# Second mixer of a two-layer trunk: heads in chunks of 128 tokens instead of 64

## The chip, the cores and the metric

The kernel runs on one core of one Trainium2 chip. The metric is the device time of one execution in microseconds (us); the kernel before took 1258.96 us, the median of three runs (1255.95 to 1259.48). The engines are named as in the profile: PE is TensorE (matrix products), PEld its loading of the stationary operand, DVE is VectorE, ACT is ScalarE, POOL is GpSimd, SP is the queue that issues the transfers.

## The reference, cut to what matters

The reference is a decoder trunk of two layers over 512 tokens and a width of 1024. The first layer has a mixer of its own and a SwiGLU part, the second the mixer below and a SwiGLU part. The second mixer has eight heads of width 128; for each head it computes a gated linear recurrence in chunks of 64 tokens:

```python
H_CHUNK = 64
def hgrn2_chunkwise(q, k, v, log_f):
    ...
    b = jnp.cumsum(log_f, axis=3)             # within the chunk
    b_last = b[:, :, :, -1:, :]
    q_inter = q * jnp.exp(b)
    k_state = k * jnp.exp(b_last - b)
    q_intra = q * jnp.exp(b - b_last)
    scores = jnp.where(causal, einsum(q_intra, k_state), 0.0)
    intra = einsum(scores, v)
    U = einsum(k_state, v)                    # what a chunk adds to the state
    decay = jnp.exp(b_last)
    def step(s, inp):
        u_c, d_c = inp
        return d_c[..., None] * s + u_c, s
    _, s_prev = lax.scan(step, zeros, (U, decay))
    inter = einsum(q_inter, s_prev)
    return intra + inter
```

The result does not depend on the chunk's length, except for rounding: a longer chunk computes more of the same sums as scores and fewer through the state.

## The kernel before, in words

All activations stand with the features on the 128 partitions and the 512 tokens along the free axis. A weight product (`prod`, `full`) splits both operands into a high and a low part of a reduced fp32 type and makes three products of 128x512 for each block of 128 features; in the profile these are the `bmm` rows with `wh`, `wl` (the parts of a weight) and `xh`, `xl` (the parts of the input), here called the wide products. The weights come by DMA into `wraw`, ACT copies the high part (`wh`), DVE (sometimes POOL) subtracts it for the low part (`wl`).

The order of the instructions on every engine is written by the planner `Sched`: tasks (generators) give a time or an event at which they may go on, and the planner picks the next one by its own table of costs. On PE it counts `p*n/2300` us for a product (`mm`; p is 4 for fp32, n the columns, at least 128 of them for fp32, and 16 for one that runs `beside` another) and 0.107 for a transpose (`tp`). The order is fixed when the program is built; on the chip an engine only waits for semaphores.

In the second mixer (`mixer1`) the wide products make `f`, `q`, `g` and `v` for the heads in the order `ORDER`. A task `gates` turns `f` and `q` of a head into `em` (named `f` in the profile: keys times a decay), `d` (named `q`: queries times a decay, for the scores), `b` (queries times a decay, for the state) and `dec` (eight decays, one for a chunk). A task `heads` then runs `head` for one head after the other, between the wide products. `head` before the change has eight chunks of 64 tokens, two in each block of 128:

- scores: 8 products of 64x64 (`bm<-q,f`), two side by side in the halves of the array, masked by DVE into `sc` (named `n`);
- transposes of the keys: 4 of 128x128 (`bs<-p,f`), copied by ACT into `kst` (also named `n`);
- state products: 7 with 64 rows (`bs<-v,n`), and with them the states `st`, one copied by ACT, six updated by DVE;
- outputs: 8 products of scores and values (`bm<-v,n`) and 7 of states and queries (`bm<-st,b`), with 64 columns of the array each;
- the norm of the outputs on ACT, DVE and POOL, and 4 transposes back (`bm<-p,n`).

A product in fp32 appears as two rows in the profile, so 8 score products are 16 rows, a transpose as one.

Of the kernel before, what the change touches and what calls it, by code (L numbers as in the profile page):

```python
# [14 lines left out]
ALU = mybir.AluOpType  # L15
# [249 lines left out]
class Kernel:  # L265
# [470 lines left out]
    def mixer1(self, nxt):  # L736
# [120 lines left out]

        def head(h, em, d, b, dec, t4, t6):

            yield t4  # L860
            ps, key = yield from self.alloc("m")
            half = [(slice(64 * u, 64 * u + 64), [slice(128 * i + 64 * u, 128 * i + 64 * u + 64) for i in range(4)])
                    for u in range(2)]
            for i in range(4):
                for u, (pp, cc) in enumerate(half):
                    t = S.mm(ps[pp, cc[i]], em[:, cc[i]], d[:, cc[i]], after=t4, beside=u > 0)
            pk, keyk = yield from self.alloc("s")
            for i in range(4):
                c = slice(128 * i, 128 * i + 128)
                tk = S.tp(pk[:, c], em[:, c], self.ident)  # L870
            sc = self.pt("n0")
            yield S.on("v", t)
            i3 = lambda z, u: z.rearrange("p (i t) -> p i t", t=128)[half[u][0], :, half[u][0]]
            for u in range(2):
                t = S.tt(i3(sc, u), i3(ps, u), self.tri[half[u][0], half[u][0]].unsqueeze(1).broadcast_to([64, 4, 64]),
                         ALU.mult, after=t)
            self.free(key)
            kst = self.pt("n5")
            tk = S.act(kst, pk, after=tk)
# [6 lines left out]
            tst = {0: 0.0}  # L886
            pu = yield from self.allocs("s", 2)
            tu = {}
            for c in (0, 1, 3, 5, 2, 4, 6):
                pp = slice(64 * (c % 2), 64 * (c % 2) + 64)  # L890
                kc = slice(128 * (c // 2), 128 * (c // 2) + 128)
                tu[c] = S.mm(pu[c % 2][0][:, kc], kst[pp, kc], v[c // 2][pp, hc])
                if c == 0:
                    tst[1] = S.act(st[:, 0], pu[0][0][:, 0:128], after=tu[0])
            yield S.on("v", max(tst[1], tu[6]))
            for c in range(1, 7):
                u = pu[c % 2][0][:, 128 * (c // 2):128 * (c // 2) + 128]
                tst[c + 1] = S.stt(st[:, c], st[:, c - 1], dec[:, c:c + 1], u, ALU.mult, ALU.add,
                                   after=max(tu[c], tst[c]))
            for g in range(2):  # L900
                self.free(pu[g][1])
# [1063 lines left out]
```

## Time and profile before

| what | value |
|---|---|
| median of three runs | 1258.96 us (1255.95 to 1259.48) |
| profiled execution, its own time | 1261.67 us |
| its span, first to last instruction | 1259.8 us |
| mean granted clock of TensorE | 0.991 of full speed |
| PE busy | 1224.8 us, 97% of the span |
| DVE busy | 720.8 us, 57% |
| ACT busy | 532.1 us, 42% |
| POOL busy | 101.6 us, 8% |
| DMA | 87 GB/s over the span |

The sums and the chain come from the profiled execution, so sums are made against its 1261.67 us. A matrix product's end is modelled in the trace, and products overlap: a duration of 0.39 us stands for a product that is followed by the next after 0.23. What a product costs is read from start to start.

### The profile page before, as it was taken

The numbers are of one execution on the slowest core, as the hardware profiler recorded it, in microseconds if no ns is written. First come the engines' busy times: TensorE is split into PE (matmuls) and PEld (weight loads), VectorE is DVE, ScalarE is ACT, GpSimd is POOL, SyncE is SP. The second block draws the span as 40 slices with busy tenths as digits, with TensorE's granted clock in tenths as the row PEclk, the third lists the DMA queues.
The fourth block names the chain that finished last, engine by engine and source line by source line (L and its number), as shares of the span: only waits on it lengthen the run. The fifth ranks groups of instructions, "written<-read, shape, count | busy, mean of one in ns | idle before, by whom it ended". The sixth has DMA issues, their size and how long they took to land.

```text
span 1259.8 us, 17687 instructions
## 1 busy us (share of the span) xinstructions
PE 1224.8 (97%) x7135; PEld 1028.4 (82%) x7135; DVE 720.8 (57%) x1225; ACT 532.1 (42%) x824; POOL 101.6 (8%) x104
## 2 busy tenths in 40 slices
PE   9988799999999999999999999999999999999996
PEld 8866689888888888889977787779988888888886
DVE  7999786863344434447766456655743444344445
ACT  5675575543322223324555455545533322223232
POOL 2200010100000000000112123310000000000002
PEclk9998999999999999999999999999999999999998
DMA  6301015142333333332132231222133333333321
GB/s 217 101 27 35 2 37 173 52 124 78 117 100 101 98 90 98 101 100 85 55 98 67 68 100 51 69 87 81 51 117 99 102 101 100 95 91 100 101 67 67
DMA packets 35072, 110.18 MB, mean 87 GB/s; under 512 B 3760, under 2 KB 6192, under 8 KB 34992
## 3 DMA queue, kind: packets, MB, share of 16 engines
q1 hardware_dynamic: 34992, 109.06, 28.4%
q8 instruction: 56, 0.92, 0.3%
q14 instruction: 24, 0.20, 0.0%
HBM read 106.95 MB, written 2.10 MB: 87 GB/s over the span
## 4 chain that ended last, share of the span: by engine, by line
PE 83%; DVE 11%; ACT 3%; issue 1%; POOL 1%; DMA 0%; SPq 0%; DVEq 0%; ACTq 0%
PE bmm L136 76%; PE bm L136 4%; PE bs L136 3%; DVE wl L156 1%; DVE n L156 1%; DVE t L156 1%; DVE xc L168 1%; POOL rcol L158 1%; DVE xl L156 1%; DVE Y L156 1%; DVE X L156 1%; DVE n L168 1%; ACT wh L150 0%; DMA wraw<-in_W_dram 0%; DVE t L172 0%
## 5 line engine op out<-in xcount | busy, mean ns | idle before, releaser
L150 ACT ACTIVATE wh<-wraw 128x1024 fp32r<-128x1024 f32 (+2 forms) x198 | 199.7, 1010 | 453.7 <-PE bmm L136 352.7
L136 PE MATMUL bmm<-xh,wh 128*128 128x512 f32 (+1 forms) x1008 | 384.4, 381 | 0.4 <-DVE Y L156 0.4
L136 PE MATMUL bmm<-xh,wl 128*128 128x512 f32 (+1 forms) x1008 | 378.5, 375 | 0.0
L136 PE MATMUL bmm<-xl,wh 128*128 128x512 f32 (+1 forms) x1008 | 378.4, 375 | 0.0
L156 DVE TENSOR_TENSOR wl<-wraw,wh 128x1024 fp32r<-128x1024 f32 (+2 forms) x196 | 228.4, 1167 | 99.7 <-ACT wh L150 99.5
L136 PEld LDWEIGHTS bmm<-xh,wh 128*128 128x128 f32 x1008 | 190.6, 189 | 37.5 <-issue 3.7
L136 PEld LDWEIGHTS bmm<-xh,wl 128*128 128x128 f32 x1008 | 190.6, 189 | 34.1
L136 PEld LDWEIGHTS bmm<-xl,wh 128*128 128x128 f32 x1008 | 190.8, 189 | 31.9
L156 DVE TENSOR_TENSOR a<-bmm,n 128x512 f32<-128x512 f32 x86 | 59.1, 691 | 219.4 <-PE bmm L136 216.2
L136 PE MATMUL bmm<-gh,wh 128*128 128x512 f32 (+1 forms) x368 | 135.0, 367 | 0.0
L136 PE MATMUL bmm<-gl,wh 128*128 128x512 f32 (+1 forms) x368 | 134.8, 366 | 0.0
L136 PE MATMUL bmm<-gh,wl 128*128 128x512 f32 (+1 forms) x368 | 134.7, 366 | 0.0
L158 POOL TENSOR_TENSOR rcol<-rstat,mhalf 128x2 f32<-128x2 f32 (+1 forms) x12 | 13.4, 1117 | 824.4 <-DVE rstat L164 824.4
L136 PEld LDWEIGHTS bmm<-gh,wh 128*128 128x128 f32 x368 | 69.4, 189 | 11.4
L136 PEld LDWEIGHTS bmm<-gl,wh 128*128 128x128 f32 x368 | 69.4, 189 | 11.3
L136 PEld LDWEIGHTS bmm<-gh,wl 128*128 128x128 f32 x368 | 69.4, 189 | 11.1
L156 DVE TENSOR_TENSOR Y<-bmm,Y 128x512 f32<-128x512 f32 (+1 forms) x40 | 23.3, 584 | 81.6 <-PE bmm L136 81.6
L150 ACT ACTIVATE xh<-X,p 128x256 fp32r<-128x256 f32 (+1 forms) x56 | 30.0, 538 | 29.7 <-DVE X L156 27.2
L150 ACT ACTIVATE n<-Y 128x256 f32<-128x256 f32 (+1 forms) x52 | 24.1, 464 | 43.5 <-DVE Y L156 42.4
L150 ACT ACTIVATE gh<-a 128x512 fp32r<-128x512 f32 x44 | 27.8, 632 | 25.9 <-DVE a L156 25.9
L148 ACT ACT_TABLE_LOAD x28 | 35.9, 1283 | 0.5
L156 DVE TENSOR_TENSOR n<-n,n 128x256 f32<-128x256 f32 (+1 forms) x44 | 23.5, 533 | 21.2 <-ACT n L150 20.9
(343 smaller groups left out, 1682.7 us busy)
## 6 DMA issues: line engine op xcount, KB each, us to landing
wraw<-in_W_dram SPq DMA_DIRECT2D x173, 512.0 KB, 3.6
wraw<-in_W_dram SPq DMA_DIRECT2D x16, 384.0 KB, 3.1
wraw<-in_W_dram SPq DMA_DIRECT2D x18, 256.0 KB, 3.0
X<-in_x_dram SPq DMA_DIRECT2D x16, 256.0 KB, 4.7
out_dram<-X SPq DMA_DIRECT2D x8, 256.0 KB, 2.2
setb<-in_s5bc_dram SPq DMA_DIRECT2D x1, 512.0 KB, 6.5
p<-in_p_dram SPq DMA_DIRECT2D x1, 226.5 KB, 6.4
n<-in_wif_dram SPq DMA_DIRECT2D x1, 192.0 KB, 4.3
```

What stands on the lines that cost most here:

```text
L136: self.nc.tensor.matmul(out, lhsT=lhsT, rhs=rhs, start=start, stop=stop, skip_group_check=True)
L148: self.nc.scalar.preload_act_table_set(t)
L150: self.nc.scalar.activation(out=out, in_=in_, func=func, scale=scale, bias=bias)
L156: self.nc.vector.tensor_tensor(out=out, in0=in0, in1=in1, op=op)
L158: self.nc.gpsimd.tensor_tensor(out=out, in0=in0, in1=in1, op=op)
L168: self.nc.vector.scalar_tensor_tensor(out=out, in0=in0, scalar=scalar, in1=in1, op0=op0, op1=op1)
```

## The change

Each head of the second mixer now works in four chunks of 128 tokens. The decays of a head are still computed by halves of 64. The scores within each half stay as they were; the cross scores of the second half against the first are four more products (`bm<-b,f`, 64x64), with the queries `b` that already hold the decay from the start of their half. The keys of the first half are scaled by the decay of the second half in place before they are transposed (three blocks, since the last chunk gives no state that is used), the queries of the second half by the decay of the first half, and the decay of a whole chunk (`whole`) is the product of two. Three states stand in place of seven. The state products and the outputs are full 128x128 products. The tile `sc` is made once for all heads; POOL fills the quarter of it that stays zero.

```diff
--- before.py
+++ after.py
@@ -855,61 +855,67 @@
                 yield from head(h, *hd.pop(h))
                 S.signal(("hd", h), 0.0)
 
+        sc = self.pt("n0")
+        S.zero(sc.rearrange("p (i t) -> p i t", t=128)[64:128, :, 0:64])
+
         def head(h, em, d, b, dec, t4, t6):
+
 
             yield t4
             ps, key = yield from self.alloc("m")
-            half = [(slice(64 * u, 64 * u + 64), [slice(128 * i + 64 * u, 128 * i + 64 * u + 64) for i in range(4)])
-                    for u in range(2)]
+            lo, hi = slice(0, 64), slice(64, 128)
+            cut = lambda i, w: slice(128 * i + w.start, 128 * i + w.stop)
             for i in range(4):
-                for u, (pp, cc) in enumerate(half):
-                    t = S.mm(ps[pp, cc[i]], em[:, cc[i]], d[:, cc[i]], after=t4, beside=u > 0)
+                for pp in (lo, hi):
+                    t = S.mm(ps[pp, cut(i, pp)], em[:, cut(i, pp)], d[:, cut(i, pp)], after=t4, beside=pp is hi)
+            yield t6
+            for i in range(4):
+                t = S.mm(ps[lo, cut(i, hi)], em[:, cut(i, lo)], b[:, cut(i, hi)], after=t6)
+            yield S.on("v", t)
+            v3 = lambda z: z.rearrange("p (i t) -> p i t", t=128)
+
+            t7 = S.tt(v3(em)[:, 0:3, lo], v3(em)[:, 0:3, lo], dec[:, 1:7:2].unsqueeze(2).broadcast_to([128, 3, 64]),
+                      ALU.mult, after=t)
+            tri = lambda pp, w: self.tri[pp, w].unsqueeze(1)
+            S.tt(v3(sc)[lo], v3(ps)[lo], tri(lo, slice(0, 128)).broadcast_to([64, 4, 128]), ALU.mult)
+            t = S.tt(v3(sc)[hi, :, hi], v3(ps)[hi, :, hi], tri(hi, hi).broadcast_to([64, 4, 64]), ALU.mult)
+            self.free(key)
+            t6 = S.tt(v3(b)[:, 1:4, hi], v3(b)[:, 1:4, hi], dec[:, 2:8:2].unsqueeze(2).broadcast_to([128, 3, 64]),
+                      ALU.mult)
+            whole = w2("whole", 2, (128, 4))
+            S.tt(whole, dec.rearrange("p (i u) -> p i u", u=2)[:, :, 0], dec.rearrange("p (i u) -> p i u", u=2)[:, :, 1],
+                 ALU.mult)
+            yield t7
             pk, keyk = yield from self.alloc("s")
-            for i in range(4):
+            for i in range(3):
                 c = slice(128 * i, 128 * i + 128)
-                tk = S.tp(pk[:, c], em[:, c], self.ident)
-            sc = self.pt("n0")
-            yield S.on("v", t)
-            i3 = lambda z, u: z.rearrange("p (i t) -> p i t", t=128)[half[u][0], :, half[u][0]]
-            for u in range(2):
-                t = S.tt(i3(sc, u), i3(ps, u), self.tri[half[u][0], half[u][0]].unsqueeze(1).broadcast_to([64, 4, 64]),
-                         ALU.mult, after=t)
-            self.free(key)
+                tk = S.tp(pk[:, c], em[:, c], self.ident, after=t7)
             kst = self.pt("n5")
-            tk = S.act(kst, pk, after=tk)
+            yield S.on("a", tk)
+            tk = S.act(kst[:, 0:384], pk[:, 0:384], after=tk)
             self.free(keyk)
             for i in range(4):
                 yield ("v", i, h // 4)
             yield tk
             st = w2("st", 1, (128, 8, 128))
             hc = slice(128 * h, 128 * h + 128)
-            tst = {0: 0.0}
-            pu = yield from self.allocs("s", 2)
-            tu = {}
-            for c in (0, 1, 3, 5, 2, 4, 6):
-                pp = slice(64 * (c % 2), 64 * (c % 2) + 64)
-                kc = slice(128 * (c // 2), 128 * (c // 2) + 128)
-                tu[c] = S.mm(pu[c % 2][0][:, kc], kst[pp, kc], v[c // 2][pp, hc])
-                if c == 0:
-                    tst[1] = S.act(st[:, 0], pu[0][0][:, 0:128], after=tu[0])
-            yield S.on("v", max(tst[1], tu[6]))
-            for c in range(1, 7):
-                u = pu[c % 2][0][:, 128 * (c // 2):128 * (c // 2) + 128]
-                tst[c + 1] = S.stt(st[:, c], st[:, c - 1], dec[:, c:c + 1], u, ALU.mult, ALU.add,
-                                   after=max(tu[c], tst[c]))
-            for g in range(2):
-                self.free(pu[g][1])
+            pu, keyu = yield from self.alloc("s")
+            tu = [S.mm(pu[:, 128 * i:128 * i + 128], kst[:, 128 * i:128 * i + 128], v[i][:, hc]) for i in range(3)]
+            yield S.on("a", tu[2])
+            tst = [S.act(st[:, 0], pu[:, 0:128], after=tu[2])]
+            yield S.on("v", tst[0])
+            for i in (1, 2):
+                tst.append(S.stt(st[:, i], st[:, i - 1], whole[:, i:i + 1], pu[:, 128 * i:128 * i + 128], ALU.mult,
+                                 ALU.add, after=tst[-1]))
+            self.free(keyu)
             po, keyo = yield from self.alloc("m")
             for i in range(4):
-                o = po[:, 128 * i:128 * i + 128]
-                yield max(t, tst[max(2 * i - 0, 0)])
-                for u, (pp, cc) in enumerate(half):
-                    S.mm(o[pp], sc[pp, cc[i]], v[i][pp, hc], start=True, stop=i + u == 0, beside=u > 0)
-                yield max(t6, tst[2 * i + 1])
+                c = slice(128 * i, 128 * i + 128)
+                yield t
+                to = S.mm(po[:, c], sc[:, c], v[i][:, hc], start=True, stop=i == 0)
                 if i > 0:
-                    S.mm(o[0:64], b[:, 128 * i:128 * i + 64], st[:, 2 * i - 1], start=False, stop=False)
-                to = S.mm(o[64:128], b[:, 128 * i + 64:128 * i + 128], st[:, 2 * i], start=False, stop=True,
-                          beside=True)
+                    yield max(t6, tst[i - 1])
+                    to = S.mm(po[:, c], b[:, c], st[:, i - 1], start=False, stop=True)
             yield S.on("a", to)
             sq = self.pt("n6")
             t = S.act(sq, po, AF.Square, after=to)
```

The order of PE for the seventh head before the change (`q`, `f` are the tiles of queries and keys, `bmm` the wide products):

```order
L136 MATMUL bm_6912<-q,f 64x64 x8
L140 MATMUL bs_6924<-p_124,f 128x128 x4
...
L136 MATMUL bs_6944<-v_5251,n_6932 128x128
L136 MATMUL bs_6945<-v_5251,n_6932 128x128
L136 MATMUL bs_6945<-v_5252,n_6932 128x128
...
L136 MATMUL bm_6966<-v_5251,n_6929 64x128 x2
L136 MATMUL bm_6966<-st,b 64x128
L136 MATMUL bm_6966<-v_5252,n_6929 64x128 x2
L136 MATMUL bm_6966<-st,b 64x128 x2
```

And after it, at the same place:

```order
L136 MATMUL bm_6848<-q,f 64x64 x8
L136 MATMUL bm_6848<-b,f 64x64 x4
...
L140 MATMUL bs_6880<-p_124,f 128x128 x3
...
L136 MATMUL bs_6895<-v_5251,n_6884 128x128
L136 MATMUL bs_6895<-v_5252,n_6884 128x128
L136 MATMUL bs_6895<-v_5253,n_6884 128x128
...
L136 MATMUL bm_6905<-v_5251,n_5276 128x128
L136 MATMUL bm_6905<-v_5252,n_5276 128x128
L136 MATMUL bm_6905<-st,b 128x128
L136 MATMUL bm_6905<-v_5253,n_5276 128x128
```

Before, the key transposes followed the scores at once; now the cross scores do, and the transposes come six wide products later (three in the second, third and sixth head), since they wait for the scaling. Three state products stand for seven, and the outputs, which had wide products in between in every head, stand in one piece in five of the eight.

The order of DVE for the same head before, from the last step of its gates (`q<-q,lf`) to the first state update:

```order
L156 TENSOR_TENSOR q<-q,lf 128x512
L156 TENSOR_TENSOR wl<-wraw,wh 128x1024
L156 TENSOR_TENSOR n_6929<-bm_6912,p_124 64x4x64 x2
L156 TENSOR_TENSOR g<-g,Y 128x512
L156 TENSOR_TENSOR f<-bmm_6864,n_5563 128x512
L156 TENSOR_TENSOR ol_5271<-g,oh_5263 128x512
L168 SCALAR_TENSOR_TENSOR st<-st,dec,bs_6945 128x128
```

And after the change:

```order
L156 TENSOR_TENSOR q<-q,lf 128x512
L156 TENSOR_TENSOR wl<-wraw,wh 128x1024
L156 TENSOR_TENSOR f<-bmm_6794,n_5565 128x512
L156 TENSOR_TENSOR g<-g,Y 128x512
L156 TENSOR_TENSOR f<-f,dec 128x3x64
L156 TENSOR_TENSOR n_5276<-bm_6848,p_124 64x512
L156 TENSOR_TENSOR n_5276<-bm_6848,p_124 64x4x64
L156 TENSOR_TENSOR b<-b,dec 128x3x64
L156 TENSOR_TENSOR whole<-dec 128x4
L156 TENSOR_TENSOR ol_5271<-g,oh_5263 128x512
L168 SCALAR_TENSOR_TENSOR st<-st,whole,bs_6895 128x128 x2
```

The evacuation of another head's `f` and the product with `g` now stand ahead of the first instruction that reads this head's scores or keys, the scaling `f<-f,dec`; before, they stood behind the masks. On POOL the fill of `sc` stands ahead of the `rcol` of the junction before the mixer. Up to the first head's scores and from the wide products behind the last head on, PE's order is the same in both.

## Rows read from the trace of the kernel before

**Rows 1.** The page, busy time by engine (us, share of the span, instructions).

```profile
PE 1224.8 (97%) x7135; PEld 1028.4 (82%) x7135; DVE 720.8 (57%) x1225; ACT 532.1 (42%) x824; POOL 101.6 (8%) x104
```

**Rows 2.** Busy time by stretch (from:to, length, engines in the page's order, clock, DMA).

```profile
640.00:820.00 180.00, 179.94 (x1058) 136.37 (x1057) 106.76 (x164) 91.92 (x132) 44.76 (x33) 1.00 0.23 72
```

**Rows 3.** PE's waits, 626 to 850 us (who, for whom: total, times, longest).

```profile
PE bm L136 <- DVE q L156: 0.5, 1, 0.5
PE bmm L136 <- DVE ol L156: 0.2, 1, 0.2
```

**Rows 4.** Order of time, PE, seventh head (start, duration, array form, operand, count).

```profile
792.14 0.39 PE L136 MATMUL bmm<-xl,wh 128*128 128x512 f32 x1
792.37 0.39 PE L136 MATMUL bmm<-xh,wl 128*128 128x512 f32 x1
792.69 0.69 PE L136 MATMUL bm<-q,f 128*64 128x64 f32 x16
793.31 0.66 PE L140 MATMUL bs<-p,f 128*128 128x128 f32 x4
793.72 0.47 PE L136 MATMUL bmm<-xh,wh 128*128 128x512 f32 x1
...
795.28 1.78 PE L136 MATMUL bs<-v,n 64*128 64x128 f32 x14
...
797.89 0.43 PE L136 MATMUL bm<-v,n 64*64 64x128 f32 x4
...
801.35 0.44 PE L136 MATMUL bm<-st,b 128*64 128x128 f32 x4
801.72 0.50 PE L136 MATMUL bmm<-xh,wh 128*128 128x512 f32 x1
802.05 0.40 PE L136 MATMUL bmm<-xl,wh 128*128 128x512 f32 x1
```

**Rows 5.** Order of time, PE, transposes back of the last head.

```profile
830.22 0.39 PE L136 MATMUL bmm<-xl,wh 128*128 128x512 f32 x1
830.45 0.39 PE L136 MATMUL bmm<-xh,wl 128*128 128x512 f32 x1
830.68 0.60 PE L140 MATMUL bm<-p,n 128*128 128x128 f32 x4
...
831.35 0.40 PE L136 MATMUL bmm<-xl,wh 128*128 128x512 f32 x1
```

**Rows 6.** Order of time, PE, full fp32 products in the first mixer.

```profile
46.38 0.40 PE L136 MATMUL bmm<-xh,wl 128*128 128x512 f32 x1
46.61 1.05 PE L136 MATMUL bm<-n,n 128*128 128x128 f32 x8
47.42 0.47 PE L136 MATMUL bmm<-xh,wh 128*128 128x512 f32 x1
47.73 0.39 PE L136 MATMUL bmm<-xl,wh 128*128 128x512 f32 x1
```

**Rows 7.** Groups by form, weight loads of the same products (busy us, mean ns).

```profile
L136 PEld LDWEIGHTS bm<-n,n 128*128 128x128 f32 x8 | 1.0, 191 | 0.1
```

**Rows 8.** Order of time, DVE, seventh head (in brackets: idle before, releaser).

```profile
790.91 0.69 DVE L156 TENSOR_TENSOR q<-q,lf 128x512 f32<-128x512 f32 x1 [1.40 <-POOL b L158]
792.98 1.23 DVE L156 TENSOR_TENSOR wl<-wraw,wh 128x1024 fp32r<-128x1024 f32 x1 [1.38 <-ACT wh L150]
794.13 0.87 DVE L156 TENSOR_TENSOR n<-bm,p 64x256 f32<-64x256 f32 x2
795.02 0.69 DVE L156 TENSOR_TENSOR g<-g,Y 128x512 f32<-128x512 f32 x1
795.75 0.69 DVE L156 TENSOR_TENSOR f<-bmm,n 128x512 f32<-128x512 f32 x1
...
797.24 1.18 DVE L168 SCALAR_TENSOR_TENSOR st<-st,dec,bs 128x128 f32<-128x128 f32 x3
```

**Rows 9.** Order of time, POOL, ahead of the second mixer.

```profile
601.73 0.69 POOL L158 TENSOR_TENSOR rcol<-rstat,mhalf 128x2 f32<-128x2 f32 x1 [4.65 <-DVE rstat L164]
```

## The prediction

> **What bounds the kernel now.** I read the page first: TensorE (PE) is busy for 1224.8 of 1259.8 us [rows 1], so a change to any other engine is worth only what it takes from or adds to PE. Then the busy times of the stretch in which the eight heads of the second mixer run, 640 to 820 us: PE is busy for 179.94 of 180.00 at full clock, VectorE (DVE) for 106.76, ScalarE (ACT) for 91.92, GpSimd (POOL) for 44.76 [rows 2]. Then PE's waits from 626 to 850 us: 0.5 us ahead of the first head's scores, 0.2 at the end of the stage [rows 3]. So the heads have no waits to be removed; what they cost is the time in which PE doesn't run the wide products (`bmm`, 512 columns) between which they stand. Since a busy PE says nothing of its pace, I read the order of time of one head on PE, start to start [rows 4].
>
> **What a head costs now.** Wide products start every 0.23 us [rows 4, 5]. In the seventh head the last one before the scores starts at 792.37, the second one after the outputs at 802.05: 9.68 us. In between lie 14 starts of wide products (that at 792.37, six, three, three, that at 801.72), 14 x 0.23 = 3.22. The head's own products therefore take 6.46 us. Its transposes back (group `bm<-p,n`, unchanged) come on top: 830.45 to 831.35 less two wide ones, 0.44 [rows 5].
>
> The rows also show why: each product is two passes (8 score products, 16 rows), and where the form of the array changes (128\*128 to 64\*128, 64\*64, 128\*64) the next product starts late, 0.32 after a wide one instead of 0.23, and the second wide one after it 0.33 instead of 0.23 [rows 4]. The outputs change form at every step, and pay 0.36 to 0.37 for each group of four passes (801.35 to 801.72).
>
> **What a full product costs.** The heads of the second mixer run none, but the first mixer does: eight passes 128\*128 over 128 columns at 46.61, between wide ones of the same form [rows 6]. They start 0.23 after the wide one, as if they were one. From 46.38 to 47.73 less two wide ones is 0.89, or 0.111 a pass, with all that entering and leaving costs.
>
> **PE, part by part, for a head after the change.**
> - Scores: 0.32 to enter and 0.62 for the 16 passes, as before [rows 4]. Cross scores add 4 products of 64 columns, 8 passes. No row has 64 columns on one half of the array alone; a pass of 128 columns takes 0.111, so half as many take 0.056 if columns set it, and 0.111 if something fixed does: 0.45 to 0.89 in all, below zero excluded since nothing is taken away for it. I take 0.45, the score passes (0.62 for eight pairs, 0.078 with the way out) being nearer to it. Back to the wide ones 0.33. Sum 0.32 + 0.62 + 0.45 + 0.33 - 0.46 = 1.26.
> - Transposes of the keys: three for four, on their own: three quarters of 0.44, 0.33.
> - State products: 3 full ones for 7 half ones, 6 passes at 0.111: 0.67 (14 passes before).
> - Outputs: 7 full ones for 15 half ones, 14 passes in one form: 1.56. In three heads they stand in two pieces; by [rows 6] entering in one form costs nothing.
>
> Sum 3.82, against 6.46: 2.64 us less a head, 21.1 for eight.
>
> **The other engines.** DVE [rows 8]: two masks of 64x256 (0.87) become one of 64x512 (0.69, as 128x512) and one of 64x256 (0.43); two scalings of 192 columns, between 0.43 for 256 and 0.39 for a 128-column update, so about 0.4 each; one of four columns, under that; and four of six state updates (1.18 for three) go. Added 1.2 to 1.5, removed 1.57: nothing, and DVE has 40% of the stretch free. ACT copies 384 columns for 512. POOL gets one fill of a 64x256 half. It waits for the same sum on PE as the `rstat` that `rcol` waits for, POOL has been idle for 4.65 us there [rows 9], and `rcol` itself takes 0.69: nothing to 0.7, and I take nothing.
>
> **What is late next.** The scaling of the keys is a new link: PE cross scores, DVE, PE transposes, with three or six wide products between. Its 0.4 fits into three wide ones (0.33 + 2 x 0.23) if DVE is free. In the seventh and eighth heads it is not: three instructions now stand between `q<-q,lf` and the scaling. In the seventh the weight split ends at 794.21 [rows 8], the evacuation of `f` takes 0.69, the product with `g` as much, the scaling 0.4: 796.0. PE would be at the transposes 1.07 + 0.33 + 5 x 0.23 after 792.69, at 795.24. So 0.5 to 0.8 in each of these two, behind which the key copy, the state products and all wide products of PE's queue stand. With 0.1 in each other head, 2.0 for eight; bounds 0 and the rival below.
>
> **Sum.** The profiled execution took 1261.67 us (span 1259.8 and 1.87 around it). 1261.67 - 21.1 + 2.0 = 1242.6. The median of the runs, 1258.96, lies 2.7 under it: 1239.9, so 1240. Outside the heads PE's order is the same; the last 216 wide products follow the last head in both, and the wait of 0.2 there [rows 3] hangs on the gate of the last `g`, not on a head.
>
> **Rivals.**
> 1. *The gain partly turns into waits (1244 to 1250).* The order on PE is written by a planner with costs of its own. It counts 0.22 for a product of 64 or 128 columns, 0.03 for one beside another, 0.11 for a transpose: 4.77 for a head before, where the chip took 6.46, so the other engines had 1.7 us a head more than planned. It counts 4.44 after the change, where I get 3.82: they have 0.6 less than planned. In the first head, with no head before it, PE did wait, 0.5 [rows 3]. If each of seven heads waits 0.6 to 1.4 at the scores or the transposes, 4 to 10 us come back: 1244 to 1250. Against: from the key transposes on, the plan (2.55) and my terms (2.56) agree, so only the scores run ahead, and a step of the plan is three wide products (0.68), which leaves a third of a microsecond on average before a wait begins.
> 2. *Slower.* If weight loads did not run under the products, a full pass would cost its load too: 0.19 [rows 7] on top of 0.111, for 20 passes a head 3.8 us, 30 for eight: 1270. The forecast's gain is gone at 0.23 a pass (19 us over 160 passes on top of 0.111). Against it speak the eight passes of [rows 6], each with a load of 0.191 [rows 7], at 0.111 start to start: loads overlap there with 128 rows in use. The Trainium skill has this rule ("TensorE: Matmul & The Clock Gate", Part 3: Packing small matmuls): loads overlap with products in flight only where the row group differs, so halves of 64 rows would hide them and full ones not; the trace contradicts it here. By the rule the sum would be 1270, by the rows 1240.
> 3. *No gain.* The stage is fed with weights no faster than now, so that PE waits for them instead. In 180 us ACT and DVE are busy for half and 60% [rows 2], and the stretches of pure wide products run at the same 0.23; so hardly. It would give 1256 to 1261.
>
> **How the numbers follow.** The forecast, 1236 to 1244 (cross scores up to 3.6 dearer, waits 0 to 4, 2 for the runs' spread): 70%. Rival 1: 22%. Rival 3: 4%, three of them within the bound below. Rival 2: 2%. Another 2% lies lower than 1236. A range of 1235 to 1249 leaves out under 2 in 10. About 0.3%, 4 us, is what a measurement can tell from no change: faster 0.95, same 0.03, slower 0.02.
>
> **What would show it.** In the changed kernel's order of time: cross scores right behind the scores, 8 passes in 0.45 (0.9 would be the fixed cost); state products and outputs as two groups of one form, 0.111 a pass, 0.23 after a wide one; waits of PE on DVE at the key transposes of the last two heads, none over 1 us. Wrong would be: passes of 0.2 or more, PE waits of over 4 us in the stretch, or a time above 1249.

## The result, and the profile after

The changed kernel takes 1243.76 us (median of four runs, 1242.3 to 1246.29) where the kernel before takes 1259.22 beside it: a ratio of 0.9884, 95% interval 0.986 to 0.9909. The forecast was 1240 with a range of 1235 to 1249. The profiled execution took 1244.7 us against 1261.67, so 17.0 less. The page of the kernel after, busy time by engine, against [rows 1]:

```profile
PE 1205.4 (97%) x6999; PEld 1026.1 (83%) x6999; DVE 718.6 (58%) x1217; ACT 531.6 (43%) x824; POOL 102.9 (8%) x105
```

PE's busy time fell by 19.4 us and DVE's sum stayed (718.6 for 720.8), as the prediction had it. Busy time by stretch, against [rows 2] (the last head now ends some 17 us earlier, so more of its work falls into the stretch):

```profile
640.00:820.00 180.00, 177.13 (x1009) 146.69 (x1010) 115.74 (x174) 97.86 (x140) 52.12 (x37) 1.00 0.25 76
```

PE is no longer busy throughout: 177.13 for 179.94. PE's waits from 626 to 850 us say where, against [rows 3]:

```profile
PE bs L140 <- DVE f L156: 2.0, 4, 0.8
PE bm L140 <- DVE n L156: 0.7, 1, 0.7
PE bm L136 <- DVE q L156: 0.5, 1, 0.5
PE bmm L136 <- DVE ol L156: 0.2, 1, 0.2
```

The last two were there before. New are four waits of the key transposes (`bs`, for the scaled keys `f`; a shorter fifth, in the fourth head, shows only start to start) and one of the transposes back (`bm`, for the normalised outputs `n`). The seventh head on PE in order of time, against [rows 4]:

```profile
779.33 0.39 PE L136 MATMUL bmm<-xh,wl 128*128 128x512 f32 x1
779.65 0.69 PE L136 MATMUL bm<-q,f 128*64 128x64 f32 x16
780.17 0.63 PE L136 MATMUL bm<-b,f 128*64 128x64 f32 x8
780.73 0.50 PE L136 MATMUL bmm<-xh,wh 128*128 128x512 f32 x1
781.06 0.39 PE L136 MATMUL bmm<-xl,wh 128*128 128x512 f32 x1
...
781.99 0.40 PE L136 MATMUL bmm<-xh,wl 128*128 128x512 f32 x1
783.06 0.55 PE L140 MATMUL bs<-p,f 128*128 128x128 f32 x3 [0.67 <-DVE f L156]
783.36 0.48 PE L136 MATMUL bmm<-xh,wh 128*128 128x512 f32 x1
783.68 0.39 PE L136 MATMUL bmm<-xl,wh 128*128 128x512 f32 x1
...
784.60 0.40 PE L136 MATMUL bmm<-xh,wl 128*128 128x512 f32 x1
784.84 0.83 PE L136 MATMUL bs<-v,n 128*128 128x128 f32 x6
...
785.74 0.39 PE L136 MATMUL bmm<-xl,wh 128*128 128x512 f32 x1
785.97 0.40 PE L136 MATMUL bmm<-xh,wl 128*128 128x512 f32 x1
786.21 0.61 PE L136 MATMUL bm<-v,n 128*128 128x128 f32 x4
...
787.55 0.39 PE L136 MATMUL bm<-st,b 128*128 128x128 f32 x2
787.69 0.47 PE L136 MATMUL bmm<-xh,wh 128*128 128x512 f32 x1
788.00 0.40 PE L136 MATMUL bmm<-xl,wh 128*128 128x512 f32 x1
```

A group between wide products is a *visit* below, and its cost is the time from the last wide start ahead of it to the second one behind it, less two wide products at 0.227. Scores with cross scores: 1.73 - 0.45 = 1.28. State products: 785.74 - 784.60 - 0.45 = 0.69. Outputs: 788.00 - 785.97 - 0.45 = 1.58. The key transposes cost 1.24 here and 0.34 where they don't wait: 0.90, although the row lists 0.67 of idle time, since the idle time is counted from the modelled end of the wide product (783.06 less 0.67 is 0.40 behind its start), where the next product would have started after 0.23. Summed so over all eight heads, the visits took 56.35 us before and 39.29 after: 17.06 less. That is the whole difference of the two executions: from the start of the last wide product ahead of the first head to the start of the last wide product of the mixer, the same two products in every kernel, PE took 231.19 us before and 214.13 after, 17.06 less again. This time is called the *stage* below.

Full products need their loads hidden. Weight loads by form, 640 to 820 us (busy us, mean ns), against [rows 7]:

```profile
L136 PEld LDWEIGHTS bm<-st,b 128*128 128x128 f32 x48 | 7.5, 192 | 0.3
L136 PEld LDWEIGHTS bs<-v,n 128*128 128x128 f32 x48 | 6.6, 191 | 0.7
```

Each load takes 0.19 us, but the passes of 786.21 to 787.55 start 0.109 to 0.114 apart: they run under the products, as [rows 6] had it.

### The profile page after: what moved, and what is told of

It is laid out like the page before. It is cut to its first block, busy times and chain, and to the rows that moved or that the text cites. A ratio compares the mean times of both kernels' runs of the same rounds, so it can differ in the third digit from the quotient of the medians.

```text
span 1242.9 us, 17436 instructions
## 1 busy us (share of the span) xinstructions
PE 1205.4 (97%) x6999; PEld 1026.1 (83%) x6999; DVE 718.6 (58%) x1217; ACT 531.6 (43%) x824; POOL 102.9 (8%) x105
## 4 chain that ended last, share of the span: by engine, by line
PE 81%; DVE 12%; ACT 3%; issue 2%; POOL 1%; DMA 0%; SPq 0%; DVEq 0%; ACTq 0%
PE bmm L136 75%; PE bm L136 3%; PE bs L136 2%; DVE wl L156 2%; DVE n L156 1%; DVE t L156 1%; ACT wh L150 1%; DVE xc L168 1%; POOL rcol L158 1%; DVE xl L156 1%; DVE Y L156 1%; ACT L148 1%; DVE X L156 1%; DVE n L168 1%; DMA wraw<-in_W_dram 0%
## 5 line engine op out<-in xcount | busy, mean ns | idle before, releaser
L156 DVE TENSOR_TENSOR n<-n,n 128x256 f32<-128x256 f32 (+1 forms) x44 | 23.5, 534 | 21.1 <-ACT n L150 20.7
```

The costliest lines, as they stand in the source:

```text
L156: self.nc.vector.tensor_tensor(out=out, in0=in0, in1=in1, op=op)
```

## The experiments

All medians, with the kernel before timed on the same chip (1258.1 to 1260.1), and the visits and the stage of one profiled execution of each (for the kernel before, 56.35 and 231.19):

| kernel | median, us (range) | ratio, 95% interval | visits, us | stage, us |
|---|---|---|---|---|
| changed kernel | 1243.76 (1242.3 to 1246.29) | 0.9884 [0.986, 0.9909] | 39.29 | 214.13 |
| again | 1242.36 (1241.45 to 1246.0) | 0.9878 [0.9861, 0.9896] | 39.28 | 214.15 |
| plan_cost | 1242.86 (1241.68 to 1244.59) | 0.9879 [0.9861, 0.9897] | 38.86 | 213.48 |
| later_visits | 1241.85 (1239.85 to 1243.02) | 0.9865 [0.9847, 0.9883] | 35.47 | 210.62 |
| cost_and_later | 1244.69 (1242.4 to 1249.23) | 0.9894 [0.9873, 0.9915] | 39.22 | 214.96 |
| scaled_early | 1241.51 (1239.64 to 1243.58) | 0.9864 [0.9844, 0.9884] | 36.07 | 210.90 |
| both_later | 1240.85 (1239.28 to 1242.11) | 0.9844 [0.9829, 0.986] | 36.19 | 210.54 |
| same_chip | 1243.35 (1242.99 to 1245.9) | 0.9872 [0.9853, 0.9891] | 39.28 | 214.14 |
| cross_twice | 1246.25 (1245.88 to 1248.05) | 0.9909 [0.9893, 0.9924] | 40.81 | 215.64 |
| out_halves | 1248.54 (1246.87 to 1249.2) | 0.9921 [0.9903, 0.9938] | 42.69 | 217.49 |
| state_halves | 1246.37 (1244.98 to 1249.7) | 0.9906 [0.9886, 0.9926] | 42.46 | 217.25 |
| halves_sorted | 1251.61 (1250.22 to 1254.9) | 0.9945 [0.9928, 0.9961] | 50.53 | 225.25 |

Differences of 3 us between medians are at the edge of what the intervals tell apart; the visits repeat far better (39.29, 39.28, 39.28 for the same kernel), and so does the stage (214.13, 214.15, 214.14). So the verdicts rest on these two, and the medians only say whether they go along.

### Is it the same each time: again, same_chip

The changed kernel, unchanged.

> The changed kernel once more, as the base for the others on the same chip. Both theories: 1242 to 1246 us, PE waits at the key transposes of five heads (1.0, 0.4, 0.4, 0.9, 0.5 us, 3.3 in all with the late start behind a wait), nothing else new.

> The changed kernel itself once more, on the same chip and beside the same runs as both_later, so that the two medians can be compared. By all theories 1242.4 to 1243.8, the visits' total 39.3 as twice before; its profiled execution may be off by 2 us outside the heads, as the first two (spans 1242.9 and 1240.6 with the same 39.3).

Medians 1242.36 and 1243.35, the same waits at the same places. The profiled spans (1242.9, 1240.6, 1241.2) differ by up to 2.3 us with equal visits: a difference of the executions, not of the heads. Most of it lies ahead of the heads, where PE's order is the same: the stage begins at 637.95, 636.09 and 636.77 us.

### Whose fault are the waits: plan_cost

```diff
-        n = 16 if beside else max(self._n(out), 32 * p)
+        n = 16 if beside else self._n(out) if narrow else max(self._n(out), 32 * p)
...
-                    t = S.mm(ps[pp, cut(i, pp)], em[:, cut(i, pp)], d[:, cut(i, pp)], after=t4, beside=pp is hi)
+                    t = S.mm(ps[pp, cut(i, pp)], em[:, cut(i, pp)], d[:, cut(i, pp)], after=t4, beside=pp is hi, narrow=True)
...
-                t = S.mm(ps[lo, cut(i, hi)], em[:, cut(i, lo)], b[:, cut(i, hi)], after=t6)
+                t = S.mm(ps[lo, cut(i, hi)], em[:, cut(i, lo)], b[:, cut(i, hi)], after=t6, narrow=True)
```

> The planner counts the 64-column products of the scores at 64 columns (0.11 us) and no longer at 128 (0.22): its scores with cross scores are then 1.0 us and not 1.9, where the chip takes 1.07. Nothing is left out. Theory A (PE reaches the key transposes too early because the plan counted the scores too dear): more wide products come between scores and transposes, the waits there fall from 3.3 us in all to under 1, time 2 to 3 us less than the changed kernel. Theory B (the scaling of the keys stands behind other DVE work, which itself follows PE, whatever the plan counts): the waits stay at 2.5 to 3.5 us, time within 1 us of the changed kernel.

Theory A was right for these waits and wrong for the time. The waits at the key transposes fell from 3.26 us (start to start, all heads) to 0.34, in the first head alone: the planner's price for scores set how many wide products stand ahead of the transposes, and with them the wait. But the time stayed: the transposes back of the third head, 1.36 us in the changed kernel, now cost 2.53. PE's waits, 600 to 860 us, and the busy times by stretch around it (engines in the page's order, clock, DMA):

```profile
PE bm L140 <- DVE n L156: 1.9, 1, 1.9
```

```profile
692.00:694.00 2.00, 0.10 (x1) 0.03 (x1) 1.70 (x4) 1.67 (x3) 1.46 (x2) 1.00 0.00 0
694.00:695.00 1.00, 1.00 (x6) 0.93 (x7) 1.00 (x1) 0.87 (x2) 0.94 (x1) 0.88 0.00 0
695.00:697.00 2.00, 2.00 (x23) 1.38 (x22) 2.00 (x3) 0.35 (x1) 0.00 (x0) 0.50 0.00 0
697.00:698.00 1.00, 1.00 (x7) 0.88 (x6) 0.81 (x3) 0.63 (x1) 0.00 (x0) 0.50 0.68 78
```

PE stood for 1.9 us and went on at 694.00 at full clock; from 695 the granted clock is 0.50, 1.2 of 2.4 GHz, and it is low for some three us in all. The scores of the fourth head fell into it: 2.60 instead of 1.29. So 2.9 us were won, 1.2 lost to the longer wait and 1.3 to the clock behind it.

### Only the order: later_visits, cost_and_later

later_visits leaves every instruction as it is and tells the planner to come back later:

```diff
-            yield t7
+            yield t7 + 1.0
...
-            yield t
+            yield t + 2.0
             pt, keyt = yield from self.alloc("m")
```

> The changed kernel, with the planner told to come back 1.0 us later for the key transposes and 2.0 us later for the transposes back than the end of DVE's step in its plan; no instruction is changed, only the order. Theory A (the waits come from the plan being too early for the chip, there is other work to fill the time): the waits of 4.2 us go, the visits' total falls to about 35, the time to about 1238-1239. Theory B (a later visit delays the next head, and DVE's queue moves along with it): the waits come back at other visits, total 38 to 40, time 1242-1244.

Theory A: no wait at any key transpose (0.34 in all eight heads), visits 35.47, 3.8 less, and the stage 3.5 less. Only the transposes back of the third head cost 0.31 too much. The ratio went from 0.9878 to 0.9865, 1.6 us, with intervals that overlap: the medians go along with the sign, not with the size, and 1241.85 is not the 1238 to 1239 that was expected.

cost_and_later has plan_cost's price and `t7 + 0.5`, `t + 2.0`.

> plan_cost (the planner counts the score and cross products by their 64 columns) together with visits planned 0.5 us later (key transposes) and 2.0 us later (transposes back); no instruction is changed, only the order. Theory A: plan_cost lost its gain at one place, a wait of 1.9 us before the transposes back of the third head, behind which TensorE's granted clock fell to 0.50 of full speed for some 2.5 us; with that visit later both go, the visits' total is about 35 and the time about 1238-1239. Theory B: the wait comes back elsewhere, total about 39, time about 1242-1243.

Theory B. The wait of 1.9 us is gone, and another of 2.9 stands before the scores of the eighth head; the clock fell behind it as well, and six wide products took 0.42 to 0.43 instead of 0.23, some 1.2 us that the visits don't hold:

```profile
802.00:803.00 1.00, 1.00 (x3) 0.74 (x3) 0.92 (x5) 1.00 (x2) 0.00 (x0) 0.50 0.00 0
```

DVE and POOL in order of time tell why PE waited (start, duration):

```profile
795.32 1.22 DVE L156 TENSOR_TENSOR wl<-wraw,wh 128x1024 fp32r<-128x1024 f32 x1
796.46 1.77 DVE L156 TENSOR_TENSOR f<-f,em 128x512 f32<-128x512 f32 x1
798.15 1.74 DVE L156 TENSOR_TENSOR q<-q,lf 128x512 f32<-128x512 f32 x1
```

```profile
795.51 2.17 POOL L158 TENSOR_TENSOR b<-q,b 128x512 f32<-128x512 f32 x1 [1.43 <-DVE g L156]
797.64 1.70 POOL L158 TENSOR_TENSOR g<-g,n 128x512 f32<-128x512 f32 x1
```

Two products of DVE that take 0.69 [rows 8] take 1.77 and 1.74 where POOL multiplies at the same time: 2.1 of the 2.9 us at most, since `q<-q,lf` writes over the tile that POOL's `b` reads until 797.68 (in [rows 8] it waits for `b`) and so could not have started before. The planner has one price for each. The Trainium skill ("SBUF — State Buffer", SBUF: two separate sides) says that a DVE operation with two inputs in SBUF and a GpSimd operation that reads SBUF need the same pair of ports, and that the one that starts first holds it for its whole instruction. The trace agrees: POOL's two end at 797.68 and 799.34, and DVE's two at 798.23 and 799.89, 0.55 behind each. It is so across the traces of all these kernels: 13 products of DVE of this size with both inputs in SBUF began while POOL was within a product of its own, and each ended 0.55 us behind POOL's; 45 that read a result of PE (`bm`, `bmm`) began so too, and took 0.68 to 0.69.

### Without the link: scaled_early, both_later

scaled_early scales the keys while the gates are made, so that no DVE instruction stands between the cross scores and the transposes:

```diff
+                ks = w2("ks", 2, (128, 3, 128))
+                t7 = S.tt(ks[:, :, 0:64], a4[:, 0:3, 0:64], dec[:, 1:7:2].unsqueeze(2).broadcast_to([128, 3, 64]),
+                          ALU.mult, after=t3)
+                t7 = max(t7, S.ts(ks[:, :, 64:128], a4[:, 0:3, 64:128], 1.0, ALU.mult, 0.0, ALU.add, after=t3))
...
+                tk = S.tp(pk[:, 128 * i:128 * i + 128], ks[:, i], self.ident, after=t7)
```

> The changed kernel, but the keys are scaled to the end of their chunk while the gates are made, into a tile of their own (two more instructions on DVE, 3*64 elements each), and TensorE transposes this tile directly behind the cross scores: no link through DVE between the two, and one visit to the full-array form less per head. Theory A (what the change did not get back is waits at the key transposes, because the scaling stands behind other work in DVE's queue): the waits of 3.3 us there go, and with one visit less the cost of one change of form (0.1 to 0.2 us per head, 0.8 to 1.6 in all); the visits' total falls from 39.3 to about 35, the time from 1242.4-1243.8 to about 1238-1239. Theory B (the heads' work is limited by DVE's total between two heads, so a wait removed comes back at the next link, as in plan_cost at the transposes back): the scaling now delays the gates' last product or the transposes back, and the visits' total stays at 38 to 40, the time at 1242-1244.

Theory A for the link: scores, cross scores and key transposes cost 1.56 as one visit, where they were 1.28 and 0.34 apart, and the waits there are gone. The visits' total fell to 36.07, not 35, since new waits stand before the scores of two heads (0.9 us of idle time) and before the transposes back of one (0.3): 1.4 us start to start, theory B's share. both_later adds `t4 + 0.8` for the scores and `t + 2.0` for the transposes back.

> scaled_early (keys scaled while the gates are made, transposed directly behind the cross scores), with the planner told to come back 0.8 us later for the scores and 2.0 us later for the transposes back: of the waits of scaled_early 1.4 us stood before the scores and 0.3 us before the transposes back. Theory A (each wait left is a visit planned before DVE's result is there, and other products fill the time): the visits' total falls from 36.1 to about 34.7, the time about 1.4 us below scaled_early's 1241.5, 3 to 4.5 us below the changed kernel on the same chip. Theory B (the wait moves to another visit): total 36 to 38, time as scaled_early's or above.

Theory B: total 36.19. The transposes back wait no more, but one wait stands before the scores of the third head and one within the outputs of the fourth (1.2 and 0.4 us of idle time, 1.27 and 0.70 start to start). Its median of 1240.85 is the lowest of all kernels here, 2.5 us below the changed kernel beside it (same_chip, 1243.35); the visits explain 3.1, and the stage is 3.6 shorter. The intervals of the two ratios overlap (0.9829 to 0.986, and 0.9853 to 0.9891), so that it beats the changed kernel is likely rather than shown.

### The price of a cross pass: cross_twice

```diff
             for i in range(4):
+                self.nc.tensor.matmul(ps[lo, cut(i, hi)], lhsT=em[:, cut(i, lo)], rhs=b[:, cut(i, hi)], start=True,
+                                      stop=True, skip_group_check=True)
                 t = S.mm(ps[lo, cut(i, hi)], em[:, cut(i, lo)], b[:, cut(i, hi)], after=t6)
```

> Each cross score product is issued twice (same operands, same target); the planner doesn't count the second, so the order of everything else stays. Theory A (in five heads PE waits for DVE at the key transposes, and DVE doesn't wait for PE): 8 more passes a head at 0.056 are 0.45 us a head, 3.6 for eight, but the five heads that wait take 2.1 of it out of their waits: 1.5 us more than the changed kernel. Theory B (the DVE work ahead of the scaling follows PE): the waits keep their size, 3.6 us more. If a pass on one half of the array has a fixed cost of 0.11, the sums are 7.2 less 3 and 7.2.

Eight more passes cost 0.467 us in every head (1.74 to 1.75 for 1.28): 0.058 for a pass of 64 columns, half of 0.111, so columns set it. 3.7 us were added and the visits grew by 1.5 only: PE comes later to the transposes, and the waits there fell from 3.3 to 1.05. The median grew more (3.9 against again's), which the heads don't hold: in the traced executions the stage is 1.5 longer, and it begins 2.3 us later (638.37 for 636.09).

### What the kernel before had lost: out_halves, state_halves, halves_sorted

Three kernels ask why halves of 64 were dear. out_halves writes each output product as two of 64 columns side by side:

```diff
-                to = S.mm(po[:, c], sc[:, c], v[i][:, hc], start=True, stop=i == 0)
+                for pp in (lo, hi):
+                    to = S.mm(po[pp, c], sc[:, cut(i, pp)], v[i][:, hc], start=True, stop=i == 0, beside=pp is hi)
```

(and the state's part alike).

> The output products are again split into two halves of 64 columns of the array (scores times values and states), two side by side, 14 products where the changed kernel has 7; rows and states stay full. Nothing is left out. Theory A (before, the outputs were dear because the form of the array changed at every step): all outputs have one form, 14 pairs of passes at 0.11 and the change of form on entering and leaving: 1.86 us a head against 1.58, 2.3 us more than the changed kernel. Theory B (full products are cheaper because they fill the array, halves are dear whatever their order): outputs cost as before, 0.36 for every four passes, 2.6 a head, 8 us more.

Outputs in one piece cost 1.89 for 1.58, and in two pieces 1.23 and 1.01 for 0.90 and 0.68: 0.31 a piece, 28 passes where 14 stood. The starts come in pairs 0.007 apart and 0.109 from pair to pair, so a pair takes as long as one full pass; what is added is entering and leaving the form. That is theory A, with visits and stage 3.4 longer where 2.3 was expected. The median grew by 6.2 against again's; the traced execution was the fastest of the four, so where the rest of the 6.2 lies is not shown. state_halves does it along the rows (the second half's products go to a bank of their own, which the states leave out):

```diff
-            tu = [S.mm(pu[:, 128 * i:128 * i + 128], kst[:, 128 * i:128 * i + 128], v[i][:, hc]) for i in range(3)]
+            tu = [[S.mm(z[:, 128 * i:128 * i + 128], kst[pp, 128 * i:128 * i + 128], v[i][pp, hc], beside=pp is hi)
+                   for z, pp in ((pu, lo), (pw, hi))][1] for i in range(3)]
```

> The changed kernel, with each state product of 128 tokens cut into two products of 64 tokens that stand behind one another on the two halves of TensorE's rows and write two banks; the second half's product is left out of the state that is summed. Six half products stand where three full ones stood. Theory A (halves side by side overlap, as the first pair of a head did in the kernel before, 0.007 us apart; what was dear before was entering and leaving the form of halves between full products): the six cost about the three full ones plus one change of form, 0.2 to 0.3 us more per head, 2 us in all, time about 1245. Theory B (a product over half of the rows costs a whole pass wherever it stands): three more of 0.23 us and the change of form, about 0.9 to 1.0 us more per head, 8 us in all, time about 1251.

Theory A, dearer than it said (0.40 a head, where 0.2 to 0.3 was expected). PE in order of time, first head:

```profile
648.38 0.39 PE L136 MATMUL bmm<-xh,wl 128*128 128x512 f32 x1
648.70 0.94 PE L136 MATMUL bs<-v,n 64*128 64x128 f32 x12
649.57 0.50 PE L136 MATMUL bmm<-xh,wh 128*128 128x512 f32 x1
649.90 0.39 PE L136 MATMUL bmm<-xl,wh 128*128 128x512 f32 x1
```

Twelve half passes take 0.87 from start to start, where the kernel before took 1.71 for fourteen (from 795.28, [rows 4], to its next wide product at 796.99); the visit costs 1.08 for 0.68. Of the 0.40 more, 0.09 is lost on entering (0.32 for 0.23); the pairs run at 0.112 but for the second, which comes 0.1 late, and the rest goes on leaving. That the kernel before paid so much more lies in the order of its halves: first, second, then two more of the second, then three of the first. Neighbours on the same half follow 0.112 apart there. The medians go along: a ratio of 0.9906 for again's 0.9878, 3.5 us, against 3.1 in the stage. halves_sorted takes the kernel before and changes this order alone:

```diff
-            for c in (0, 1, 3, 5, 2, 4, 6):
+            for c in range(7):
...
+            yield t
             for i in range(4):
                 o = po[:, 128 * i:128 * i + 128]
-                yield max(t, tst[max(2 * i - 0, 0)])
                 for u, (pp, cc) in enumerate(half):
                     S.mm(o[pp], sc[pp, cc[i]], v[i][pp, hc], start=True, stop=i + u == 0, beside=u > 0)
+            for i in range(4):
+                o = po[:, 128 * i:128 * i + 128]
                 yield max(t6, tst[2 * i + 1])
```

In this order all four sums of a bank are started before the first is added to, and the outputs come out other than in the kernel before; count and form of the products are the same.

> The kernel before, chunks of 64 tokens, with the same products in another order: the seven state products alternate between the halves of 64 rows (they stood as first, second, second, second, first, first, first half), and the outputs run all eight score products first and then the seven state products, so that the array's form changes once instead of seven times. Theory A (what the kernel before lost was changes of form and neighbours on the same half; a half product beside one of the other half costs half of a full one): state products from 1.92 to about 1.3 us per head (four pairs at 2*0.112 and the change of form, by state_halves 0.39), outputs from 3.4 to about 2.4 (eight pairs' time for both kinds of products, 16*0.112, one more change of form than in out_halves); 1.6 us less per head, 13 in all: time about 1246, three quarters of what the whole change brought. Theory B (the gain came from full products, which need half as many passes): the order brings little, under 0.4 us per head, time 1256-1260.

Between the two: 7.4 us of 13, the visits 5.8 less. Outputs fell from 3.38 to 2.65 us per head (2.4 expected). The state products stayed at 1.92, for a reason that neither theory had. PE in order of time, first head, and its waits from 626 to 850 us:

```profile
648.52 0.49 PE L136 MATMUL bs<-v,n 64*128 64x128 f32 x4
649.38 0.93 PE L136 MATMUL bs<-v,n 64*128 64x128 f32 x10 [0.36 <-ACT st L150]
650.24 0.50 PE L136 MATMUL bmm<-xh,wh 128*128 128x512 f32 x1
650.57 0.40 PE L136 MATMUL bmm<-xl,wh 128*128 128x512 f32 x1
```

```profile
PE bs L136 <- ACT st L150: 3.0, 8, 0.5
```

The third product writes the bank of the first, which ACT is still copying: 0.36 us of idle time and a new start in each head. The old order had put three products into the other bank meanwhile. The first four passes would take some 0.32, so some 0.54 of the 0.86 from 648.52 to 649.38 is the wait: an estimate of 1.38 without it, close to the 1.3 expected.

## Why the prediction was right, and where it was short

The chain it named is the one that the runs show: the visits of the eight heads hold the whole difference (17.06 us of the stage), and nothing moved outside them. Its terms, per head:

| term | predicted | measured | shown by |
|---|---|---|---|
| scores and cross scores | 1.26 | 1.28 | cross pass at 64 columns 0.058, where 0.056 was taken (cross_twice) |
| key transposes, without wait | 0.33 | 0.34 | seven heads of plan_cost and all of later_visits |
| state products | 0.67 | 0.68 | every head |
| outputs | 1.56 | 1.58 | every head; two pieces (0.90 and 0.68) cost no more than one |
| waits, eight heads together | 2.0 | 4.2 | later_visits: 3.8 go when the visits come later |

- **The gain.** 8 x 2.64 = 21.1 us were forecast. Measured are 17.06 less in the visits, and 4.16 of waits in them: 21.2 without the waits. The four terms came out 0.06 a head dearer than taken, and the heads before cost 6.53 on average (without the first one's old wait), where the seventh, which was read, cost 6.46; the two misses cancel.
- **Why it is there.** The prediction said passes; out_halves, state_halves and halves_sorted say more exactly what. Halves that alternate take as long in a pair as one full pass (0.109 to 0.112 a pair), so a full product saves time only over halves that don't alternate. The other part is changes of form, 0.3 to 0.4 for each group that stands in another form than its neighbours. In the state products the change brought 1.24 us a head, of which the form makes 0.40 (state_halves). In the outputs, doing with one change between halves what seven did brought 0.73 of the 1.80 us that the change brought; no run divides the other 1.07. The Trainium skill ("TensorEngine Tiling (Array Packing)", Key Properties) has both halves of this, that tiles work in parallel and that a change of mode drains the engine; the trace agrees, with 0.007 us between starts in a pair and 0.3 to 0.4 for a group.
- **The step that was mis-sized: the waits.** The prediction took 0.5 to 0.8 in the seventh and eighth heads and 0.1 in the others. Start to start it was 0.90 and 0.53 there, and 1.03, 0.43 and 0.37 in the first, third and fourth heads, 3.26 in all at this place. The reading of the seventh head's queue was right. DVE, order of time:

```profile
780.07 1.47 DVE L156 TENSOR_TENSOR wl<-wraw,wh 128x1024 fp32r<-128x1024 f32 x1 [0.78 <-ACT wh L150]
781.46 0.68 DVE L156 TENSOR_TENSOR f<-bmm,n 128x512 f32<-128x512 f32 x1
782.06 0.68 DVE L156 TENSOR_TENSOR g<-g,Y 128x512 f32<-128x512 f32 x1
782.66 0.35 DVE L156 TENSOR_TENSOR f<-f,dec 128x192 f32<-128x192 f32 x1
```

The three instructions that were named (split, evacuation, product with `g`) stand ahead of the scaling `f<-f,dec`. In the first head it is others, which the prediction didn't follow. DVE again:

```profile
639.86 1.23 DVE L172 TENSOR_TENSOR_SCAN b<-seg,lf 128x512 f32<-128x512 f32 x1 [0.70 <-ACT lf L150]
641.12 0.92 DVE L156 TENSOR_TENSOR lf<-b 128x512 f32<-128x512 f32 x1
641.96 0.35 DVE L156 TENSOR_TENSOR f<-f,dec 128x192 f32<-128x192 f32 x1
```

The gates of the next head stand there: a scan that waits for ACT, and a product. The prediction took 0.1 for a head in which no queue had been read. In the fourth head, products for `g` and `ol` stand ahead of the scaling. In the third it is no queue at all: DVE stood idle until the cross scores came, but the scaling itself, taken at 0.4 and measured at 0.35 elsewhere, took 1.13 beside a product on POOL:

```profile
680.33 1.13 DVE L156 TENSOR_TENSOR f<-f,dec 128x192 f32<-128x192 f32 x1 [0.23 <-PE bm L136]
```

```profile
679.51 1.73 POOL L158 TENSOR_TENSOR q<-q,n 128x512 f32<-128x512 f32 x1 [2.30 <-ACT n L150]
```

POOL ends at 681.24 and the scaling at 681.46; it took 1.13 in again and same_chip too, 0.77 in cross_twice, where less of POOL's product was left, and 0.36 in later_visits, where POOL had ended. This is the collision that cost_and_later shows, and neither the prediction nor a rival had it.
- **The wait that it had not at all**: 0.9 us before the transposes back of the third head, where `n<-bm,ss` stands on DVE behind an evacuation that itself waits for PE:

```profile
693.29 0.69 DVE L156 TENSOR_TENSOR g<-bmm,n 128x512 f32<-128x512 f32 x1 [1.58 <-PE bmm L136]
693.90 0.68 DVE L156 TENSOR_TENSOR g<-g,Y 128x512 f32<-128x512 f32 x1
694.50 0.68 DVE L156 TENSOR_TENSOR n<-bm,ss 128x512 f32<-128x512 f32 x1
```

```profile
692.83 1.01 POOL L158 TENSOR_TENSOR ss<-ss,mhalf 128x4 f32<-128x4 f32 x1
```

DVE was idle for 1.58 us with `ss` still to come from POOL. It came at 693.84, but DVE had begun two instructions that stand ahead of `n`, which therefore started at 694.50: 0.66 us later, most of PE's idle time of 0.7.
- **From 1240 to 1243.76.** The waits make 2.2. The profiled execution of before lay 2.7 us over its median, and the prediction took this off; that of after lies 0.9 over its own: 1.8, chance of the executions and no part of the mechanism. The terms give 0.1 back.
- **Rival 1** (gain partly into waits) was the right mechanism: the planner did overcount the scores, and plan_cost, which mends that, took the waits at this link away (the 0.9 at the transposes back it did not). It was priced at 4 to 10 us for seven heads and cost 4.2 in six places, so the time fell where the two cases meet. **Rival 2** (loads not overlapped, 1270, after the rule that the prediction weighed) is refuted by 0.19 us loads under passes 0.11 apart, in 20 passes a head. **Rival 3** (no gain) fell with the time.
- **The signs it named.** The cross scores and the groups of one form came as described. The waits did not stay in the last two heads. Start to start the longest is 1.03 us, where none over 1 was named, and their sum is 4.2, just over the 4 us that were to count against it; as idle time they are 0.8 and 2.9 us.
- **The fill on POOL**, taken at nothing, cost nothing: PE's wait for POOL's `rcol` ahead of the second mixer is 0.8 us in both kernels.

## What to carry to other kernels

Price a matrix product of half the array by its neighbours: halves that alternate cost together what a full one costs, halves of the same side follow one another, and here each group in another form pays 0.3 to 0.4 us, so sort by form before rewriting the tiling, and look which bank each product writes. When a busy engine gets faster, read the queue of the engine it waits for next in every repetition, not only in one, and look what runs beside it on POOL; the waits taken from a queue that was read were right to 0.3 us, and those taken at a flat 0.1 made the miss. A plan with one price for each instruction can trade a wait for a worse one elsewhere (plan_cost, cost_and_later): judge an order by the sum of the waits on the chip.

## What was not expected of the hardware

- Behind waits of PE of 1.9 and 2.9 us the granted clock fell to half (1.2 GHz) only after PE had gone on, by an estimate from the mean clock of the microsecond in which it fell (0.88 and 0.69) some 0.8 and 1.4 us after, for about three; behind waits of up to 1.2 us (both_later) it stayed at 1.00 in the stretch of the heads. The late fall hits the work that follows, not the wait.
- DVE's products of 128x512 took up to 1.79 us instead of 0.69 when they began while POOL multiplied, and ended 0.55 us behind POOL's each time; those that read a result of PE were not slowed.
- Passes of opposite halves start 0.007 us apart; a full fp32 pass over 128 columns and a pair of halves both take 0.11.
